# Rows of a modulation, sums of u and sigmoids moved between the stages of a decoder block's token mixer

## The chip, the cores and the metric

The kernel runs on one NeuronCore of a Trainium2 chip. Its time is the device time of one execution in microseconds (us). Five engines work side by side, each with its own queue in program order: PE (TensorE, matmuls; PEld loads their weights), DVE (VectorE, elementwise work on two operands), ACT (ScalarE, copies and functions with one operand), POOL (GpSimd) and SP (SyncE, which issues the DMAs here). Semaphores tie the queues together. On-chip data lie in SBUF, and matmuls write to eight PSUM banks of 128 x 512 floats.

## The reference

A decoder block of width 1024 over 512 tokens: a first SwiGLU network, a token mixer and a second SwiGLU network, each behind an RMSNorm with a modulation that a vector c sets (shift, scale and gate, nine vectors of 1024 in all), then a last RMSNorm. What matters here:

```python
mod = cond @ w_ada[l] + b_ada[l]                      # 9 x 1024 values, 72 groups of 128
sh1, sc1, gt1, sh2, sc2, gt2, sh3, sc3, gt3 = ...
u = modulate(rmsnorm(h, g_norm_mix[l]), sh2, sc2)
h = h + gt2 * token_mixing(u, ...)
...
def token_mixing(u, ...):
    proj = u @ w_in                                   # p (256), q, k, v (768 each), gate logits (2 x 1024)
    y_pool = multiscale_pool(p, w_pool, pool_scale)   # trailing means over 2, 4, 8, 16 tokens
    # rotary q and k; three groups of four heads: window 128, and dilations 4 and 16
    y_attn = ...                                      # merged by the groups' softmax denominators
    gates = jax.nn.sigmoid(gate_logits)
    g_pool, g_attn = jnp.split(gates, 2, axis=-1)
    merged = g_pool * (y_pool @ w_pool_branch) + g_attn * (y_attn @ w_attn_branch)
    return merged @ w_out
```

## The kernel before

Activations lie feature by feature on the partitions: u is eight tiles of 128 features x 512 tokens. Every matmul is done in three: each fp32 operand is split into a high part (rounded to the fp32r format, a copy on ACT) and a low part (the difference, on DVE), and high x high, high x low and low x high are summed (`mm3`, L360 to L362). So each weight chunk of 128 x 1024 that SP loads into a buffer (`raw`, three of them) costs ACT an instruction (L317, into `whi`) and DVE one (L329, into `wlo`). PE runs without a break almost everywhere; DVE is the next busiest. Nothing is scheduled by a planner: the order on each engine is the order in which the Python code records instructions. Work for DVE and ACT is put beside PE's matmuls by hooks, called ahead of the k-th step of a product tile (`mm_tile`, eight steps of three matmuls).

The mixer (`mix`, `merge_out`) goes through these stages, in PE's order:

- first values: four tiles of v for the first head group, with the rotary steps (`rope_b`, L1058 and L1059) of the first q and k beside them; the shifted copies for these are made by DMAs from `v23` (L1050);
- eight product tiles of q and k for the groups two and three, with attention units of the first group in their hooks at step 5: values (L1147), transposes of the probabilities (L1129), scores (L1096), and DVE's and ACT's softmax (`at_exp`, L1112 to L1117);
- two tiles for the pooling, whose trailing sums POOL makes (`pool_diff`, L1219 to L1228);
- values by class: four tiles, one for each residue class of the tokens (L1380 to L1382), each copied from its bank into `v23` by DVE (L1386), with the units of groups two and three in their hooks at step 5. The unit's values (L1147) in the tile of class c+1 read the copy of class c;
- four gate tiles (output tiles 6 and 7, gates for pooling and attention), and beside them the merge of the groups' softmax (`at_merge`), pooling's map (`pool_map`) and the attention's output (`at_spread` on PE, `at_y` on DVE and ACT);
- the gated merge (`merge_out`): for each output tile a branch of 12 matmuls (`branch`) and, for six of the eight, the gates by pairs in a product of the Strassen kind with seven products of 24 narrow matmuls instead of eight (`gate_duo`, L747 to L749);
- output product: five full tiles, then three in two halves of the tokens (`out_tail`), in which the sums of squares for the next norm are gathered in `AR` (L440, L557) and read by PE (`stats_t`, L450).

Three kinds of work are spread over these stages and matter here.

A row of the modulation: 512 KB of `w_ada` are loaded into a free tile (`ada_fetch`, L379), and DVE multiplies it with the condition and sums it up in one instruction of 128 x 1024 (`ada_do`, L387). `bg` does one row and fetches ahead by `ada_depth`; every eight rows a group is closed by one or two small instructions (`ada_fin`, L400 to L404). Rows 48 to 63 are done in the mixer up to the values by class (`ada_stop` 64), 64 to 71 in the output product.

Sums of u: the seven products need sums and differences of u's four quarters, split in two parts again. `mix_sums` returns them as a list of steps that `nxt` takes off one at a time: L977 adds two parts, L987 subtracts, L981 (ACT) and L985 (DVE) split. Its scratch tiles x are q and k tiles that are free late.

Sigmoids: the four gate tiles stay in PSUM, and `merge_out` applies the sigmoid to all four at one point (`sigmoids`, L1487), with ACT's table load ahead of them.

In the duo the first product's bank A is copied on ACT to C and reused (L1407); PE's third and fifth product, which add to A, wait for such copies.

Of the kernel before, what the change touches and what calls it, by code (L numbers as in the profile page):

```python
# [14 lines left out]
P = 128  # L15
T = 512
# [130 lines left out]
class Kernel:  # L147
# [234 lines left out]
    def ada_do(self, j, n=1, between=None):  # L382
        t, mod = self.adat.pop(j), self.mod[:, j:j + 1]
        for i in range(n):
            c = slice(i * D // n, (i + 1) * D // n)
            o = self.part if i else mod
            self.nc.vector.scalar_tensor_tensor(t[:, c], t[:, c], 1.0, self.cond[:, c], op0=OP.mult, op1=OP.mult,  # L387
                                                accum_out=o)
# [4 lines left out]
        if self.ada_free is not None and not any(t is x for x in self.ada_gone):  # L393
            self.ada_free.append(t)
# [799 lines left out]
    def at_y(self, banks):  # L1194
        nc, v = self.nc, self.nc.vector
        for hp in range(2):
            x, y = self.o1[:, hp, :], self.o23[:, hp, :]
            v.tensor_tensor(x, x, banks[2 * hp], op=OP.mult)
            v.tensor_tensor(y, y, banks[2 * hp + 1], op=OP.mult)
            v.tensor_tensor(x, x, y, op=OP.add)  # L1200
            nc.scalar.activation(self.YH[hp], x, AF.Copy)
            v.tensor_tensor(self.YL[hp], x, self.YH[hp], op=OP.subtract)
# [28 lines left out]
    def pool_map(self):  # L1231

        nc = self.nc
        banks = (self.bO, self.bS[0])
# [10 lines left out]
    def mix(self):  # L1245
# [7 lines left out]
        two = lambda pool, n, dt=F32R: [pool.tile([P, T], dt, name=f"{n}{i}") for i in range(2)]  # L1253
        self.PH, self.PL, self.YH, self.YL = (two(mp, n) for n in ("PH", "PL", "YH", "YL"))
        ma = outer.enter_context(tc.tile_pool(name="ma", bufs=1))
        with tc.tile_pool(name="rt", bufs=1) as self.rt, tc.tile_pool(name="aw", bufs=2) as self.aw, \
# [19 lines left out]
            self.ada_free, self.ada_stop, self.ada_depth = [self.AR], 64, 2  # L1276
# [15 lines left out]
            for n in range(4):  # L1292
# [59 lines left out]

            self.ada_gone = mine
            self.ada_free = [x for x in self.ada_free if not any(x is y for y in mine)] + [self.cs]
            self.ada_depth = 1
            b = self.mm_tile(hooks(g23[0], [(2, lambda: by_class(1)), (3, self.bg), (7, self.bg)]))
            self.pool_diff(1, b)
            wide = lambda pool, n: lambda: pool.tile([P, D], F32R, name=n)
# [7 lines left out]
            sums, last = self.mix_sums([self.qt[2], self.qt[1], self.kt[1]], [[wide(ma, "k2"), wide(mp, "uc")],  # L1366
                                       [wide(ma, "v1"), wide(ma, "k0")], [lambda: half(0), lambda: half(1)]])
            nxt = lambda: sums.pop(0)()
            self.held = self.pos
            w = [x for _ in range(4) for x in self.take()]  # L1370
            for c in range(4):
                mid = [lambda c=c: by_class(c + 1)] if c in (1, 2) else []
                hk = hooks(g23[c + 1], [(7, self.bg)], mid) if c < 3 else \
                    hooks([], [(2, self.at_swap), (2, nxt), (3, nxt), (6, nxt), (7, nxt)])
                b = self.nb()
                for k in range(KT):
# [6 lines left out]
                    if k == 4:  # L1383
# [4 lines left out]
            assert self.ada_next == 64 and not self.adat, self.ada_next  # L1388
            gates = [self.mm_tile(hooks([], [(1, nxt), (3, nxt), (5, self.at_merge)]))]
            v.memset(self.fT.bitcast(F32), 0.0)  # L1390
            v.tensor_tensor(self.sel.rearrange("p (j d) -> p j d", j=8),
                            *(self.ident[:64, r:r + 8, None].to_broadcast([64, 8, 64]) for r in (0, 32)), op=OP.add)
            gates.append(self.mm_tile({1: [nxt], 3: [nxt], 6: [self.pool_map, lambda: self.at_fT(self.bS[1])]}))
# [7 lines left out]
        self.merge_out(gates, last, ma)  # L1401
# [42 lines left out]
    def merge_out(self, ready, last, ma):  # L1444
        nc, tc = self.nc, self.tc
        v = nc.vector
        with tc.tile_pool(name="mg", bufs=1) as mg:
# [15 lines left out]
            def branch(m):  # L1463
                gp, ga = (x[:, m % 2 * T:(m % 2 + 1) * T] for x in sc)
                self.look()
# [13 lines left out]
                def parts():  # L1479
                    nc.scalar.activation(MH[m], gp, AF.Copy)  # L1480
# [4 lines left out]
            def sigmoids():  # L1485
                for i, b in enumerate(ready):
                    nc.scalar.activation(sc[i % 2][:, i // 2 * T:(i // 2 + 1) * T], b, AF.Sigmoid)  # L1487


            rest = [sigmoids]  # L1490
            do = lambda n=1: [rest.pop(0)() for _ in range(n)]

            place(tile_of(ma, "q1"), 6)
            place(tile_of(ma, "k1"), 7)
# [34 lines left out]
            for m in range(5):  # L1529
# [6 lines left out]
                self.bg()  # L1536
                if m < 3:
                    self.bg()
# [7 lines left out]
    def build(self):  # L1546
# [39 lines left out]
        self.ada_free, self.ada_depth, self.ada_gone = None, 3, []  # L1586
# [189 lines left out]
```

## Time and profile before

| | |
|---|---|
| Median of 3 runs | 995.04 us (992.8 to 995.55) |
| The profiled execution | 994.62 us, of which the span from the first to the last instruction is 992.8 |
| Granted TensorE clock | 1.000 |
| PE busy | 981.1 us, 99% of the span |
| DVE busy | 787.2 us, 79% |
| ACT busy | 475.3 us, 48% |
| POOL busy | 32.3 us, 3% |
| The mixer in the span | from about 360 to 645 us |
| POOL's sums | 452 to 480 us |

How to read the rows: a timeline row gives the start in us from the span's start, the time in us, engine, line, operation, out<-in by the program's names, shapes, and in brackets the engine's idle time before it and what ended it. The next instruction of DVE can start some 0.08 us before the row of the last one ends. A row of the waits view gives who waited for whom: us in total, times, longest. A row of the DMA view ends with the median us from issue to landing. `bank` stands for any PSUM bank, and `k`, `q`, `v`, `uc` for tiles of that name, which later hold other things (sums of u, merged halves).

### The profile page before, as it was taken

How to read it: one execution, taken by the hardware profiler on the slowest of the kernel's cores; microseconds unless marked ns; L12 is line 12 of the kernel's file. 1: busy time of each engine (PE TensorE's matmuls, PEld its weight loads, DVE VectorE, ACT ScalarE, POOL GpSimd, SP SyncE). 2: the span in 40 equal slices, each digit the busy share in tenths (PEclk: the TensorE clock that was granted, in tenths of full speed). 3: DMA queues.
4: the chain of work that ended last, by engine and by line, in shares of the span. 5: the costliest groups of instructions: out<-in, count | busy, mean ns of one | idle time of the engine just before them, and what ended most of it. 6: DMA issues, size and time to landing. Idle time of an engine off the chain costs nothing.

```text
span 992.8 us, 16356 instructions
## 1 busy us (share of the span) xinstructions
PE 981.1 (99%) x6686; PEld 893.3 (90%) x6686; DVE 787.2 (79%) x1091; ACT 475.3 (48%) x713; POOL 32.3 (3%) x31
## 2 busy tenths in 40 slices
PE   8999999999999999999999999999999999999997
PEld 7888998989999899787878998998899899998997
DVE  7989979889797676889888876868787776676764
ACT  6453653625435554455535553455365254352553
POOL 0000000000000000007300000000000000000002
PEclk9999999999999999999999999999999999999999
DMA  9856446455563415655133325522344134241312
GB/s 344 277 187 236 150 149 193 147 194 169 182 197 111 135 56 194 195 198 199 61 101 114 104 67 195 190 64 90 103 152 133 55 111 144 85 150 43 105 45 85
DMA packets 44876, 141.74 MB, mean 143 GB/s; under 512 B 6273, under 2 KB 9089, under 8 KB 44802
## 3 DMA queue, kind: packets, MB, share of 16 engines
q1 hardware_dynamic: 44226, 140.18, 43.4%
q8 instruction: 52, 0.85, 0.4%
q10 hardware_dynamic: 576, 0.52, 0.2%
q14 instruction: 22, 0.18, 0.1%
HBM read 135.29 MB, written 2.24 MB: 139 GB/s over the span
## 4 chain that ended last, share of the span: by engine, by line
PE 87%; DVE 6%; ACT 2%; issue 2%; DMA 2%; SPq 0%; POOL 0%; POOLq 0%; DVEq 0%; ACTq 0%
PE bank L360 14%; PE bank L361 14%; PE bank L362 14%; PE bank L747 13%; PE bank L748 12%; PE bank L749 12%; PE bank L1702 1%; PE bank L1704 1%; PE bank L1706 1%; DVE wlo L329 1%; DMA H<-xT 1%; DVE ut L467 1%; PE bank L1147 1%; DVE UL L493 1%; PE bank L1096 0%
## 5 line engine op out<-in xcount | busy, mean ns | idle before, releaser
L329 DVE TENSOR_TENSOR wlo<-raw,whi 128x1024 fp32r<-128x1024 f32 (+4 forms) x162 | 172.8, 1079 | 49.7 <-ACT whi L317 49.4
L747 PE MATMUL bank<-UH,whi 128*128 128x256 f32 x640 | 176.8, 276 | 0.0
L748 PE MATMUL bank<-UL,whi 128*128 128x256 f32 x640 | 176.8, 276 | 0.0
L749 PE MATMUL bank<-UH,wlo 128*128 128x256 f32 x640 | 176.8, 276 | 0.0
L317 ACT ACTIVATE whi<-raw 128x1024 fp32r<-128x1024 f32 (+4 forms) x162 | 146.3, 921 | 57.6 <-DVE raw L261 54.1
L360 PE MATMUL bank<-HI,whi 128*128 128x512 f32 (+1 forms) x406 | 146.2, 360 | 0.0
L361 PE MATMUL bank<-HK,whi 128*128 128x512 f32 (+1 forms) x406 | 145.9, 359 | 0.0
L362 PE MATMUL bank<-HI,wlo 128*128 128x512 f32 (+1 forms) x406 | 145.8, 359 | 0.0
L329 DVE TENSOR_TENSOR wlo<-X,whi 128x1024 fp32r<-128x1024 f32 (+3 forms) x104 | 112.0, 1084 | 31.8 <-ACT whi L317 31.5
L747 PEld LDWEIGHTS bank<-UH,whi 128*128 128x128 f32 x640 | 120.2, 188 | 0.4
L748 PEld LDWEIGHTS bank<-UL,whi 128*128 128x128 f32 x640 | 120.2, 188 | 0.0
L749 PEld LDWEIGHTS bank<-UH,wlo 128*128 128x128 f32 x640 | 120.2, 188 | 0.0
L747 PE MATMUL bank<-SH,whi 128*128 128x256 f32 x408 | 112.7, 276 | 0.0
L748 PE MATMUL bank<-SL,whi 128*128 128x256 f32 x408 | 112.6, 276 | 0.0
L749 PE MATMUL bank<-SH,wlo 128*128 128x256 f32 x408 | 112.6, 276 | 0.0
L317 ACT ACTIVATE whi<-X 128x1024 fp32r<-128x1024 f32 (+3 forms) x104 | 95.7, 943 | 34.4 <-DVE X L261 33.7
L360 PE MATMUL bank<-UH,whi 128*128 128x512 f32 (+1 forms) x304 | 105.6, 347 | 0.0
L361 PE MATMUL bank<-UL,whi 128*128 128x512 f32 (+1 forms) x304 | 104.2, 343 | 0.1
L362 PE MATMUL bank<-UH,wlo 128*128 128x512 f32 (+1 forms) x304 | 104.0, 342 | 0.0
L362 PEld LDWEIGHTS bank<-HI,wlo 128*128 128x128 f32 x406 | 76.2, 188 | 11.7
L360 PEld LDWEIGHTS bank<-HI,whi 128*128 128x128 f32 x406 | 76.2, 188 | 11.5
L361 PEld LDWEIGHTS bank<-HK,whi 128*128 128x128 f32 x406 | 76.3, 188 | 11.3
(336 smaller groups left out, 1842.4 us busy)
## 6 DMA issues: line engine op xcount, KB each, us to landing
raw<-wmix SPq DMA_DIRECT2D x44, 512.0 KB, 3.8
raw<-wf1i SPq DMA_DIRECT2D x31, 512.0 KB, 4.3
raw<-wf2i SPq DMA_DIRECT2D x30, 512.0 KB, 4.4
ada<-wada SPq DMA_DIRECT2D x23, 512.0 KB, 5.7
AR<-wada SPq DMA_DIRECT2D x18, 512.0 KB, 4.6
cs<-wada SPq DMA_DIRECT2D x14, 512.0 KB, 3.7
X<-wf2i SPq DMA_DIRECT2D x14, 512.0 KB, 3.7
X<-wf1i SPq DMA_DIRECT2D x12, 512.0 KB, 4.3
```

The costliest lines, as they stand in the source:

```text
L317: self.nc.scalar.activation(self.hi[:, y], r[:, x], AF.Copy)
L329: self.nc.vector.tensor_tensor(self.lo[:, y], r[:, x], self.hi[:, y], op=OP.subtract)
L360: M(ps, hi, uh, start=start, stop=False)
L361: M(ps, hi, ul, start=False, stop=False)
L362: M(ps, lo, uh, start=False, stop=stop)
L467: self.nc.vector.scalar_tensor_tensor(t[:, hs], self.H[k][:, hs], G, self.Rn[hs.start][:, hs], op0=OP.mult, op1=OP.mult)
L493: self.nc.vector.scalar_tensor_tensor(self.UL[k][:, hs], t[:, hs], S, self.UH[k][:, hs], op0=OP.add, op1=OP.subtract)
L747: M(o, hi, uh, start=start and p == 0 and k == 0, stop=False, skip_group_check=True)
L748: M(o, hi, ul, start=False, stop=False, skip_group_check=True)
L749: M(o, lo, uh, start=False, stop=k == 3, skip_group_check=True)
L1147: self.nc.tensor.matmul(self.bO[64 * h:64 * h + 64, P * hp:P * hp + P], x, pt[:, (2 * h + j) * P:(2 * h + j + 1) * P], start=j == first, s ...
L1702: M(b, hi, self.UH[k], start=k == 0, stop=False)
```

## The change

It does four things.

1. Rows. A tile `uc` is added to the free tiles for the first rows, and one row is done beside each of the last three of the four first values (three rows instead of one). The mixer stops at row 61 instead of 64: the eight q and k tiles keep one row each and the first pooling tile two, and the rows in the second pooling tile (two) and in the first three classes (one each) are gone. The output product does 11 rows (3, 3, 2, 2, 1 beside its full tiles) instead of 8 (2, 2, 2, 1, 1).
2. Sums of u. They start in the second pooling tile instead of the fourth class: two steps there, two each in the first and second class, three in the fourth, and one or two in the gate tiles. Their scratch is three tiles of the pool `mx` that later hold PH, YH and YL (so these become two halves of one tile), and q2. The constants for the spread (`fT`, `sel`) are made beside the third class.
3. Sigmoids. Each gate tile has its sigmoid beside a later gate tile; the result goes into q1 and k1, and the merge of output tiles 6 and 7 reads it from there. The tiles for the merged halves 6 and 7 are placed when they are written.
4. `at_y` makes both high parts before both low parts.

PE's instructions and their order are the same in both kernels.

```diff
     def mix_sums(...):
         def last():
-            u = x[0].rearrange("p (k t) -> p k t", k=4)
+            u = x[3].rearrange("p (k t) -> p k t", k=4)
...
-        return [lambda: whole(b, 0, 1), lambda: whole(x[0], 4, 1),
-                lambda: (v.tensor_tensor(x[0], x[0], b, op=OP.add), hi(0)), lambda: whole(x[1], 0, 0),
-                lambda: sub(x[2], x[1], b), lambda: (sub(x[1], x[0], x[1]), lo(0)),
-                lambda: (hi(2), whole(x[0], 4, 0)), lambda: (hi(1), sub(x[0], x[0], x[1])), lambda: lo(2), lambda: lo(1)], last
+        return [lambda: whole(b, 0, 1), lambda: whole(x[0], 4, 1), lambda: v.tensor_tensor(x[0], x[0], b, op=OP.add),
+                lambda: whole(x[1], 0, 0), lambda: sub(x[2], x[1], b), lambda: sub(x[1], x[0], x[1]),
+                lambda: (hi(0), whole(x[3], 4, 0)), lambda: lo(0), lambda: sub(x[3], x[3], x[1]), lambda: hi(1),
+                lambda: hi(2), lambda: lo(2), lambda: lo(1)], last
...
     def at_y(self, banks):
...
             nc.scalar.activation(self.YH[hp], x, AF.Copy)
-            v.tensor_tensor(self.YL[hp], x, self.YH[hp], op=OP.subtract)
+        for hp in range(2):
+            v.tensor_tensor(self.YL[hp], self.o1[:, hp, :], self.YH[hp], op=OP.subtract)
...
     def mix(self):
+        x = [mp.tile([P, D], F32, name=n) for n in ("PH", "YL", "YH")]
...
-            self.ada_free, self.ada_stop, self.ada_depth = [self.AR], 64, 2
+            uf = mp.tile([P, D], F32, name="uc")
+            self.ada_free, self.ada_stop, self.ada_depth = [self.AR, uf], 61, 2
...
+                if n == 1:
+                    self.ada_free += [self.v23.rearrange("p n f -> p (n f)")[:, i * D:(i + 1) * D] for i in range(2)]
+                if n:
+                    self.bg()
                 if n == 2:
-                    mine = [self.v23.rearrange("p n f -> p (n f)")[:, i * D:(i + 1) * D] for i in range(2)]
-                    self.ada_free += mine
-                    self.bg()
+                    self.ada_free = [t for t in self.ada_free if t is not uf]
...
-            b = self.mm_tile(hooks(g23[0], [(2, lambda: by_class(1)), (3, self.bg), (7, self.bg)]))
+            sums, last = self.mix_sums(x + [self.qt[2]], ...)
+            b = self.mm_tile(hooks(g23[0], [(2, lambda: by_class(1)), (3, nxt), (7, nxt)]))
...
-                hk = hooks(g23[c + 1], [(7, self.bg)], mid) if c < 3 else \
-                    hooks([], [(2, self.at_swap), (2, nxt), (3, nxt), (6, nxt), (7, nxt)])
+                hk = hooks(g23[c + 1], [(2, nxt), (7, nxt)] if c < 2 else [(2, clear)], mid) if c < 3 else \
+                    hooks([], [(2, self.at_swap), (2, nxt), (3, nxt), (6, nxt)])
...
-            gates = [self.mm_tile(hooks([], [(1, nxt), (3, nxt), (5, self.at_merge)]))]
-            v.memset(self.fT.bitcast(F32), 0.0)
-            v.tensor_tensor(self.sel...)
+            gates = [self.mm_tile(hooks([], [(5, self.at_merge), (7, nxt)]))]
...
-            gates.append(self.mm_tile({1: [nxt], 3: [nxt], 4: [lambda: self.at_spread(spread)]}))
+            at = [t[:, i * T:(i + 1) * T] for t in (self.qt[1], self.kt[1]) for i in range(2)]
+            sig = lambda i: lambda: nc.scalar.activation(at[i], gates[i], AF.Sigmoid)
+            gates.append(self.mm_tile({1: [nxt, sig(0)], 2: [sig(1)], 4: [lambda: self.at_spread(spread)]}))
             self.at_y(spread)
-            gates.append(self.mm_tile())
+            gates.append(self.mm_tile({1: [sig(2)]}))
+            sig(3)()
...
     def merge_out(...):                 # branch(m)
+                sp, sa = (gp, ga) if m < 6 else (ready.pop(0), ready.pop(0))
...
-                    v.tensor_tensor(gp, gp, pb, op=OP.mult)
-                    v.tensor_tensor(ga, ga, ab, op=OP.mult)
+                    v.tensor_tensor(gp, sp, pb, op=OP.mult)
+                    v.tensor_tensor(ga, sa, ab, op=OP.mult)
...
-            rest = [sigmoids]
+            rest = []
...
                 self.sumsq(m, self.H[m])()
-                self.bg()
-                if m < 3:
+                for _ in range((3, 3, 2, 2, 1)[m]):
                     self.bg()
```

L996 of the changed kernel, which the prediction names, is the third step of `mix_sums` there, the sum of x[0] and b.

More of the change, by code (lines that the diff above doesn't have):

```diff
@@ L392, in ada_do @@
                 between()
-        if self.ada_free is not None and not any(t is x for x in self.ada_gone):
+        if self.ada_free is not None:
             self.ada_free.append(t)
@@ L1229, in pool_diff, with pool_map @@
         self.pd[t] = d
-    def pool_map(self):
+    def pool_map(self, high, low):
         nc = self.nc
+        self.PH, self.PL = high, low
         banks = (self.bO, self.bS[0])
@@ L1252, in mix @@
         mp = outer.enter_context(tc.tile_pool(name="mx", bufs=1))
-        two = lambda pool, n, dt=F32R: [pool.tile([P, T], dt, name=f"{n}{i}") for i in range(2)]
-        self.PH, self.PL, self.YH, self.YL = (two(mp, n) for n in ("PH", "PL", "YH", "YL"))
+        x = [mp.tile([P, D], F32, name=n) for n in ("PH", "YL", "YH")]
+        two = lambda n: [t[:, i * T:(i + 1) * T] for t in [mp.tile([P, D], F32R, name=n)] for i in range(2)]
+        wide = lambda pool, n: lambda: pool.tile([P, D], F32R, name=n)
         ma = outer.enter_context(tc.tile_pool(name="ma", bufs=1))
@@ L1351, in mix @@
             self.pool_diff(0, b)
-            self.ada_gone = mine
-            self.ada_free = [x for x in self.ada_free if not any(x is y for y in mine)] + [self.cs]
-            self.ada_depth = 1
-            b = self.mm_tile(hooks(g23[0], [(2, lambda: by_class(1)), (3, self.bg), (7, self.bg)]))
-            self.pool_diff(1, b)
-            wide = lambda pool, n: lambda: pool.tile([P, D], F32R, name=n)
+            assert self.ada_next == 61 and not self.adat, self.ada_next
             v4 = []
@@ L1364, in half, with clear @@
                 return v4[0][:, i * D:(i + 1) * D]
-            sums, last = self.mix_sums([self.qt[2], self.qt[1], self.kt[1]], [[wide(ma, "k2"), wide(mp, "uc")],
+            sums, last = self.mix_sums(x + [self.qt[2]], [[wide(ma, "k2"), wide(mp, "uc")],
                                        [wide(ma, "v1"), wide(ma, "k0")], [lambda: half(0), lambda: half(1)]])
             nxt = lambda: sums.pop(0)()
+            b = self.mm_tile(hooks(g23[0], [(2, lambda: by_class(1)), (3, nxt), (7, nxt)]))
+            self.pool_diff(1, b)
             self.held = self.pos
             w = [x for _ in range(4) for x in self.take()]
+            def clear():
+                v.memset(self.fT.bitcast(F32), 0.0)
+                v.tensor_tensor(self.sel.rearrange("p (j d) -> p j d", j=8),
+                                *(self.ident[:64, r:r + 8, None].to_broadcast([64, 8, 64]) for r in (0, 32)), op=OP.add)
             for c in range(4):
                 mid = [lambda c=c: by_class(c + 1)] if c in (1, 2) else []
-                hk = hooks(g23[c + 1], [(7, self.bg)], mid) if c < 3 else \
-                    hooks([], [(2, self.at_swap), (2, nxt), (3, nxt), (6, nxt), (7, nxt)])
+                hk = hooks(g23[c + 1], [(2, nxt), (7, nxt)] if c < 2 else [(2, clear)], mid) if c < 3 else \
+                    hooks([], [(2, self.at_swap), (2, nxt), (3, nxt), (6, nxt)])
                 b = self.nb()
@@ L1387, in mix @@
             self.held = None
-            assert self.ada_next == 64 and not self.adat, self.ada_next
-            gates = [self.mm_tile(hooks([], [(1, nxt), (3, nxt), (5, self.at_merge)]))]
-            v.memset(self.fT.bitcast(F32), 0.0)
-            v.tensor_tensor(self.sel.rearrange("p (j d) -> p j d", j=8),
-                            *(self.ident[:64, r:r + 8, None].to_broadcast([64, 8, 64]) for r in (0, 32)), op=OP.add)
-            gates.append(self.mm_tile({1: [nxt], 3: [nxt], 6: [self.pool_map, lambda: self.at_fT(self.bS[1])]}))
+            gates = [self.mm_tile(hooks([], [(5, self.at_merge), (7, nxt)]))]
+            pool_map = lambda: self.pool_map(two("PH"), two("PL"))
+            gates.append(self.mm_tile({1: [nxt], 3: [nxt], 6: [pool_map, lambda: self.at_fT(self.bS[1])]}))
             rest = [b for b in self.banks if b not in gates] + [self.bS[0]]
@@ L1584, in build @@
         self.scr2 = dram.tile([32, 2 * T], F32, name="scr2")
-        self.ada_free, self.ada_depth, self.ada_gone = None, 3, []
+        self.ada_free, self.ada_depth = None, 3
         with self.open_ffn():
```

10 lines of the change are left out of this document (4 added, 6 removed).

## The prediction

> **What bounds the kernel now.** I read the page first, then PE's waits between 420 and 680 us (the stretch that the change touches), then the rows around each wait, engine by engine.
>
> ```profile
> span 992.8 us, 16356 instructions
> PE 981.1 (99%) x6686; PEld 893.3 (90%) x6686; DVE 787.2 (79%) x1091; ACT 475.3 (48%) x713; POOL 32.3 (3%) x31
> ...
> PE bank L747 <- ACT bank L1407: 1.3, 1, 1.3
> PE bank L1147 <- DVE v L1386: 0.8, 1, 0.8
> PE bank L747 <- ACT gc L1407: 0.6, 1, 0.6
> ```
>
> PE is busy for 99% of the span, so only PE's own waits can be won, and any new wait of PE is paid in full. In this stretch there are three of note, and behind each stands DVE's queue, directly or through ACT. PE runs the same 6501 instructions in the same order in both kernels; the change moves DVE, ACT and SP instructions against them.
>
> ```profile
> 469.90 1.09 PE L1147 MATMUL bank<-probT,v 128*64 128x128 f32 x16 [0.85 <-DVE v L1386]
> ...
> 526.69 0.28 PE L747 MATMUL bank<-k,whi 128*128 128x256 f32 x1
> ...
> 529.30 0.28 PE L749 MATMUL bank<-k,wlo 128*128 128x256 f32 x1
> 530.92 0.39 PE L747 MATMUL bank<-v,whi 128*128 128x256 f32 x1 [1.35 <-ACT bank L1407]
> 531.14 0.28 PE L748 MATMUL bank<-k,whi 128*128 128x256 f32 x1
> ...
> 533.73 0.28 PE L749 MATMUL bank<-v,wlo 128*128 128x256 f32 x1
> ...
> 536.56 0.28 PE L749 MATMUL bank<-UH,wlo 128*128 128x256 f32 x1
> 537.45 0.39 PE L747 MATMUL bank<-v,whi 128*128 128x256 f32 x1 [0.61 <-ACT gc L1407]
> ```
>
> Counted from start to start, the second wait costs 529.30 to 530.92 less one step, 1.5 us, the third 536.56 to 537.45 less one step, 0.8. A wait also leaves a slower beat: 23 steps from 526.69 to 529.30 are 0.1135 each, 22 from 531.14 to 533.73 are 0.1177. Over the five products of 24 narrow matmuls that follow in this duo that is another 0.5.
>
> **The duo's waits (gain).** What made DVE and ACT late there:
>
> ```profile
> 511.65 0.63 ACT L1201 ACTIVATE YH<-o 128x512 fp32r<-128x512 f32 x1 [5.55 <-DVE o L1200]
> 520.06 1.28 ACT L1487 ACT_TABLE_LOAD   x1
> ...
> 523.28 1.08 ACT L317 ACTIVATE whi<-cs 128x1024 fp32r<-128x1024 f32 x1
> ...
> 528.71 1.15 ACT L317 ACTIVATE whi<-raw 128x512 fp32r<-128x512 f32 x2 [3.40 <-DVE raw L261]
> ...
> 530.29 0.58 ACT L1407 ACTIVATE bank<-bank 128x512 f32<-128x512 f32 x1
> ...
> 518.18 0.39 PE L362 MATMUL bank<-UH,wlo 128*128 128x512 f32 x1
> ...
> 524.39 1.23 DVE L329 TENSOR_TENSOR wlo<-cs,whi 128x1024 fp32r<-128x1024 f32 x1 [3.05 <-ACT whi L317]
> 527.46 1.22 DVE L261 TENSOR_TENSOR raw<-raw,raw 128x1024 f32<-128x1024 f32 x1
> ```
>
> Table load and four sigmoids hold ACT from 520.06 to 523.28, between the high part of AR and that of cs. DVE waits 3.05 us for the latter, so its raw<-raw comes at 527.46, ACT's high part at 528.71, and the copy of A's bank, which PE needs at 529.4, ends at 530.87. After the change the table load and two sigmoids fall into ACT's 5.55 us of idle time before 511.65; the other two stand ahead of AR's high part, and the last waits for the last gate tile, whose matmuls end at 518.6. So AR's high part goes from 519.0 to about 519.3, but that of cs from 523.28 to about 520.3, and the whole chain behind it comes 2.9 us earlier: raw<-raw at 524.6, the copy ends at 528.0. PE no longer waits at 529.4, and the third wait's copy comes 2.9 earlier against 2.3 that PE itself gains, a margin of about 0.4. The low parts YL, now behind both halves, no longer wait for ACT each; that lies ahead of the same chain and isn't counted again. Gain 1.5 + 0.8 + 0.5 = 2.75, the upper bound; the lower is 1.5, if the third wait stays. Fewer sums in the gate tiles give nothing of their own: the output of the attention there waits for PE's spread matmuls.
>
> **First values (loss).** Three modulation rows instead of one stand here. The last rotary step, which the first scores read, now has two rows ahead of it instead of one.
>
> ```profile
> 392.31 0.69 DVE L1059 TENSOR_TENSOR k<-k,k 128x512 f32<-128x512 f32 x1
> ...
> 393.57 0.71 PE L1096 MATMUL bank<-k,q 64*128 64x128 f32 x8
> ...
> 396.72 0.39 ACT L1117 ACTIVATE prob<-prob,negmax 128x128 f32<-128x128 f32 x1
> ...
> 399.80 0.60 PE L1129 MATMUL bank<-cst,prob 128*128 128x128 f32 x4
> ...
> 611.83 1.22 DVE L387 SCALAR_TENSOR_TENSOR k<-k,cond 128x1024 f32<-128x1024 f32 x1
> ...
> 612.97 1.22 DVE L387 SCALAR_TENSOR_TENSOR k<-k,cond 128x1024 f32<-128x1024 f32 x1
> ```
>
> A row costs DVE 1.14 from start to start (611.83 to 612.97). The rotary step ends at 393.00, 0.57 before PE's scores; handing over takes 0.14 (a copy of v ends at 469.76, PE starts at 469.90). So 1.14 - 0.43 = 0.7 us of new wait; bounds 0 and 1.1. DVE is then 2.3 late, PE 0.7; the probabilities have 2.7 us until their transposes (397.11 to 399.80), which covers the difference of 1.6, and DVE's waits for loads and scores up to 440 take it up. The two loads more on SP's queue stand before and among the shifted copies, long before they are used; the weights' first load behind them stays first.
>
> **Values by class (loss).** Five rows leave, and u's sums come in their place, one for one, but for one: in the first class a sum at its third step (L996) is added ahead of the copy of v that PE waits for already.
>
> ```profile
> 462.46 3.47 DVE L329 TENSOR_TENSOR wlo<-raw,whi 128x1024 fp32r<-128x1024 f32 x2 [1.46 <-ACT whi L317]
> ...
> 469.08 0.68 DVE L1386 COPY v<-bank 128x512 f32<-128x512 f32 x1
> ...
> 476.48 0.68 DVE L1386 COPY v<-bank 128x512 f32<-128x512 f32 x1
> ...
> 462.67 2.17 POOL L1228 TENSOR_TENSOR k<-k,tr 64x512 f32<-64x512 f32 x1
> ...
> 474.10 1.29 POOL L1228 TENSOR_TENSOR k<-k,v 64x512 f32<-64x512 f32 x1
> ...
> 478.82 0.44 PE L1147 MATMUL bank<-probT,v 128*64 128x128 f32 x4
> ```
>
> DVE's queue is full from 462.46 to that copy, and its idle 1.46 before can't take the sum, which stands behind the low part that waits for ACT. So the copy comes later by at least 1.14. Beside POOL such an instruction took up to 2.3 us (two low parts 3.47, of which 1.2 is what one takes alone), and POOL's own was stretched from 1.29 to 2.17: they take turns. With one more DVE instruction there, the low part behind it meets POOL's next one. I take 2.0, nearer the slow rows since POOL has work at nearly every moment there; bounds 1.1 and 3.2.
>
> [...]
>
> In the second class two sums replace one row: 1.14 against 478.82 - 477.16 - 0.14 = 1.5 of slack, so nothing; one more turn of POOL's would make it 0.6 to 0.8. From there on DVE has less to do than before, and POOL's differences, later too, are read only in the gate tiles.
>
> **Output product (loss).** Eleven rows instead of eight stand here, all ahead of the last sum of squares of the first half, which PE reads at 639.99, and with them the two small instructions that close the group of the first 64 rows.
>
> ```profile
> 611.16 0.75 DVE L1534 SCALAR_TENSOR_TENSOR H<-bank,mod,H 128x512 f32<-128x512 f32 x1 [4.60 <-PE bank L362]
> ...
> DVE AR L440 <- ACT ut L439: 2.9, 4, 0.8
> ...
> 632.68 0.09 DVE L387 DVE_READ_ACCUMULATOR k<-k,cond 128x1 f32 x1
> ...
> 633.08 0.48 DVE L516 SCALAR_TENSOR_TENSOR H<-bank,mod,H 128x256 f32<-128x256 f32 x1
> ...
> 638.40 0.42 DVE L557 TENSOR_TENSOR AR<-AR,gc 128x256 f32<-128x256 f32 x1
> ...
> 639.99 0.60 PE L450 MATMUL bank<-ones,AR 128*128 128x128 f32 x4
> ...
> k<-wada SPq DMA_DIRECT2D x6, 512.0 KB, 6.2
> ```
>
> From 611.16, where PE released it, to 638.82 DVE waits for nothing but four times for ACT's square of its own result (2.9 us together, and these waits stay). Three rows are 3.4 us, the closing pair 0.4 (its like stands between 632.68 and 633.08). The slack at the sum is 639.99 - 638.82 - 0.14 = 1.0. PE waits 2.8; with 0.1 for a row whose load is late, 2.9. A load needs 6.2 us in the median and three tiles rotate, so at three rows a tile one may be 1.5 late: bounds 1.5 and 4.4. The weights' loads behind the rows on SP's queue come 2 to 3 us later, but ACT's use of them is later by as much.
>
> **Sum.** 994.62 (the profiled execution; its span 992.8 and 1.8 around it) + 0.7 + 2.0 + 2.9 - 2.75 = 997.5 us, 0.25% over the median 995.04, which lies 0.4 over the profiled one. All other work is the same. A measurement of this kernel can tell about 0.3% (3.0 us) from no change, so the sum is a loss just inside it. From the bounds: 994.62 + 0 + 1.1 + 1.5 - 2.75 = 994.5 to 994.62 + 1.1 + 4.0 + 4.4 - 1.5 = 1002.6.
>
> **Rivals.**
> A, faster: DVE takes the added work in its own waits (2.9 before L440, 1.46 before 462.46). Then no new wait arises and the by-class one of 0.85 goes with its rows: 994.62 - 2.75 - 0.85 = 991.0. Against it: those waits stand behind instructions fixed in order.
> B, the output product's rows are hidden: the sum is done before PE asks, which needs 2.8 of 3.8 us found elsewhere. 997.5 - 2.9 = 994.6. For it: DVE idles for 4.6 us before 611.16; against it: the rows stand behind that instruction.
> C, slower: POOL's turns. If in the first two classes L996 and the sums behind it each wait out one POOL instruction (about 1.0 each), both copies of v are late: by-class 2.0 becomes 3.2, the second class adds 0.8, and 0.5 more where the third follows. 997.5 + 2.5 = 1000.0. It decides from the second extra turn on. For it: the row of 3.47; against it: with the first class later, POOL is nearly done when the second comes.
> D, the change doesn't do what it says: the fourth sigmoid waits for the last gate tile ahead of AR's high part. If that delay is 3 us rather than 0.3, the copies come as late as now: 997.5 + 2.75 = 1000.2.
> E, PE's clock falls after the longer waits (2.9 each, at the first class and at the sum of squares). The granted clock is 1.00 in every row, beside a wait of 1.35 too. At half rate for as long as each wait lasts, 1.45 each: 1000.4. [...]
>
> **Chances.** Forecast 0.46, its own range 995.5 to 999.2, of which the part over 998.0 (0.15) is slower and the rest (0.31) the same. A 0.12, B 0.12, C 0.19, D 0.07, E 0.04. Faster: A less a sliver, 0.11. Same: 0.31 + 0.12 + 0.01 = 0.44. Slower: 0.15 + 0.19 + 0.07 + 0.04 = 0.45. The range 993.0 to 1001.0 holds the forecast and B to E and leaves out A and the outer ends of C and E, about 0.17.
>
> **What would show it.** PE's wait before the values of the second class grows from 0.85 to 2.9; the two waits on L1407's copies are gone and the beat stays at 0.1135; a new wait of 2.8 stands before L450, released by DVE's L557; one of 0.7 before the first L1096. It is wrong if L450 or the first class shows no new wait (then A or B), if a copy of A's bank still holds PE (D), or if the granted clock leaves 1.00 (E).

## The result and the profile after

The changed kernel takes 996.36 us in the median against 994.15 for the kernel before, both over 22 runs: a ratio of 1.0023, with a 95% interval of 1.0016 to 1.0029. It is 2.2 us slower, which is inside the 0.3% that count as no change here. The forecast was 997.5. The profiled execution took 995.25, only 0.63 more than that of the kernel before, so 1.6 of the 2.2 isn't in this first trace; it is looked for below.

The page of the changed kernel, its span and PE's row:

```profile
span 993.5 us, 16359 instructions
PE 981.3 (99%) x6686; PEld 893.9 (90%) x6686; DVE 787.3 (79%) x1091; ACT 475.3 (48%) x713; POOL 33.9 (3%) x31
```

PE's waits between 380 and 680 us (what waits, for what, us in all, how often, the longest):

```profile
PE bank L450 <- DVE AR L557: 2.6, 1, 2.6
PE bank L1147 <- DVE v L1396: 0.9, 1, 0.9
...
```

Busy times are nearly the same; the waits have moved. Both waits on ACT's copies in the duo are gone, the one before the values of the second class has kept its size, and a new one of 2.6 stands before L450. The rows behind this, from the timeline (start, duration, instruction; in brackets the wait before it and who ended it):

```profile
393.85 0.69 DVE L1059 TENSOR_TENSOR k<-k,k 128x512 f32<-128x512 f32 x1
393.98 1.11 PE L1096 MATMUL bank<-k,q 64*128 64x128 f32 x8
...
470.76 1.09 PE L1147 MATMUL bank<-probT,v 128*64 128x128 f32 x16 [0.90 <-DVE v L1396]
...
519.45 0.60 ACT L1406 ACTIVATE k<-bank 128x512 f32<-128x512 f32 x1 [3.06 <-PE bank L362]
...
520.89 1.05 ACT L317 ACTIVATE whi<-cs 128x1024 fp32r<-128x1024 f32 x1
...
528.06 0.58 ACT L1419 ACTIVATE bank<-bank 128x512 f32<-128x512 f32 x1
530.14 0.28 PE L749 MATMUL bank<-k,wlo 128*128 128x256 f32 x1
530.25 0.28 PE L747 MATMUL bank<-v,whi 128*128 128x256 f32 x1
...
640.07 0.42 DVE L557 TENSOR_TENSOR AR<-AR,gc 128x256 f32<-128x256 f32 x1
640.54 0.71 PE L450 MATMUL bank<-ones,AR 128*128 128x128 f32 x4 [2.59 <-DVE AR L557]
```

- First values: the eight scores take 1.11 from the first to the end instead of 0.71. The first four start on time, since they read the earlier rotary step; the other four wait for the one that ends at 394.54.
- Duo: the last sigmoid waits for its gate tile and ends at 520.05; the high part of cs starts at 520.89 instead of 523.28, though PE is 0.84 later there than in the kernel before (the first three rows of the table below). The copy of A's bank ends at 528.64, and PE goes from 530.14 to 530.25 without a break.
- Output product: the last sum of squares ends at 640.49, and PE has been idle since 638.0.

PE runs the same 6686 matmuls in the same order in both kernels (the 6501 of the prediction stands in no view), so one can subtract the starts of the same instruction. How much later (+) PE gets through each stretch, from the profiled executions; the third and fourth columns compare further executions (e1 and e4, below) with the first one of the changed kernel:

| stretch of the kernel before, us | changed - before | e1 - changed | e4 - changed |
|---|---|---|---|
| 0 to 390 (start, first network) | +0.41 | -0.68 | -0.55 |
| 390 to 400 (first values) | +0.40 | 0.00 | 0.00 |
| 400 to 529 (values by class, gate tiles) | +0.03 | -0.01 | +0.02 |
| 529 to 600 (duos) | -3.03 | 0.00 | 0.00 |
| 600 to 645 (output product) | +2.81 | +1.59 | +2.15 |
| 645 to the end | +0.01 | +0.03 | 0.00 |
| sum | +0.63 | +0.93 | +1.62 |

The first row is no part of the change: the start differs by such amounts between executions (by 0.2 between two of the kernel before, by 0.7 between two of the changed one). The rest sums to +0.22, far from the 2.2 of the medians.

### The profile page after: what moved, and what is told of

Read it like the earlier page. It is cut to its first block, busy times and chain, and to the rows that moved or that the text cites. A ratio compares the mean times of both kernels' runs of the same rounds, so it can differ in the third digit from the quotient of the medians.

```text
span 993.5 us, 16359 instructions
## 1 busy us (share of the span) xinstructions
PE 981.3 (99%) x6686; PEld 893.9 (90%) x6686; DVE 787.3 (79%) x1091; ACT 475.3 (48%) x713; POOL 33.9 (3%) x31
## 4 chain that ended last, share of the span: by engine, by line
PE 83%; DVE 8%; DMA 3%; SPq 2%; ACT 2%; issue 2%; POOL 0%; POOLq 0%; DVEq 0%; ACTq 0%
PE bank L747 13%; PE bank L748 13%; PE bank L749 13%; PE bank L360 12%; PE bank L361 12%; PE bank L362 12%; DVE wlo L329 2%; SPq L1050 1%; PE bank L1710 1%; PE bank L1712 1%; PE bank L1714 1%; DMA v<-wada 1%; DMA rt<-tr 1%; DVE k L387 1%; DVE v L387 1%
```

## The experiments

Eleven runs. e1 to e4 stood beside runs of the kernel before with a median of 994.33, e5 to e8 beside 994.74, e9 to e11 beside 994.46.

**e1: the changed kernel again.**

> The changed kernel unaltered, for a second profiled execution. Question: the two traces shown differ by 0.63 us at PE's end, the medians by 2.2. If the profiled execution was only a quick one of the same kind (theory: no cost is missing, the executions vary), this one shows PE's waits at the same places with the same sizes (0.9 before the values of the second class, 2.6 before L450) and a ratio of about 1.0022. If a cost is missing from that trace (rival: the granted clock falls after the wait of 2.6 in most executions, since most ran at a mean clock of 0.997 and this profile at 0.999), a profile with a mean clock of 0.997 shows a stretch of a clock under 1.00 behind L450 and 1 to 2 us of slower matmuls there.

997.39, ratio 1.0029 (1.0019 to 1.0040). All waits are where they were, with the wait before L450 at 2.5. But behind it PE is slower. Windows of 1 us of this execution (length, PE's busy time and matmuls, granted clock, share of the DMA engines, GB/s):

```profile
639.00:640.00 1.00, 0.19 (x1) 1.00 0.63 205
640.00:641.00 1.00, 1.00 (x10) 0.99 0.87 266
641.00:642.00 1.00, 1.00 (x7) 0.50 0.69 131
642.00:643.00 1.00, 1.00 (x6) 0.50 0.78 311
643.00:644.00 1.00, 1.00 (x7) 0.50 0.13 53
644.00:645.00 1.00, 1.00 (x9) 0.80 0.00 0
645.00:646.00 1.00, 1.00 (x10) 1.00 0.42 25
```

The windows behind the same wait in the first execution of the changed kernel:

```profile
640.00:641.00 1.00, 0.46 (x4) 1.00 0.75 164
641.00:642.00 1.00, 1.00 (x11) 1.00 0.69 274
642.00:643.00 1.00, 1.00 (x11) 1.00 0.63 250
643.00:644.00 1.00, 1.00 (x11) 1.00 0.71 291
```

In e1 the clock stands at half from 640.98 to 644.40 (worked out from 0.99 and 0.80 in the end windows), 3.42 us, and 6 or 7 matmuls go through in a microsecond instead of 11. That is the +1.59 of the table. e4, below, has the same fall, from 640.4 to 643.8. The mean clock of an execution is a sign of it: 0.997 or less in 17 of the 22 runs of the result and in all 8 of e1, never under 0.998 in the 63 runs of the kernel before beside the experiments. It is a rough sign: the clock also falls at the end of a trace (from 992.26 of 992.8 in the kernel before, from 991.43 of 993.5 in the changed one, worked out from windows of 0.2 us), and the profiled execution of e8, below, has a mean of 0.998 with 1.00 in every window from 635 to 647. The rival holds: this cost was missing from the first trace.

**e2: three rows early.** DVE is idle from 604.4 to 609.0 ahead of the first product's result, and the first loads have landed by then.

```diff
             do()
+            for _ in range(3):
+                self.bg()
             bs = [self.nb(), self.nb()]
...
-                for _ in range((3, 3, 2, 2, 1)[m]):
+                for _ in range((2, 2, 2, 1, 1)[m]):
```

> Three of the eleven rows of the output product stand ahead of its first product's read, in DVE's idle stretch from 604.4 to 609.0 (three rows take 3.4; the third load landed at 606.8), eight behind as before the change. Theory (the three extra rows are the whole of the new wait before L450): that wait of 2.6 is gone or under 0.3, 2.7 us less than the changed kernel, 993.7, ratio 0.9995 to the kernel before; if the clock falls because of that wait, another 1 less, 992.7 (0.9985). Rival (the wait comes from ACT's squares or the loads that come late behind the rows): the wait stays at 1.5 or more, ratio above 1.001.

991.93, ratio 0.9973 (0.9962 to 0.9984): 4.4 less than the changed kernel in the result, 5.5 less than e1 on the same chip, and 2.4 less than the kernel before beside it. The timeline of e2:

```profile
603.73 1.22 DVE L387 SCALAR_TENSOR_TENSOR k<-k,cond 128x1024 f32<-128x1024 f32 x1
...
606.02 1.22 DVE L387 SCALAR_TENSOR_TENSOR v<-v,cond 128x1024 f32<-128x1024 f32 x1
...
608.41 0.75 DVE L1545 SCALAR_TENSOR_TENSOR H<-bank,mod,H 128x512 f32<-128x512 f32 x1 [0.76 <-PE bank L362]
...
636.48 0.41 DVE L557 TENSOR_TENSOR AR<-AR,gc 128x256 f32<-128x256 f32 x1
637.24 0.60 PE L450 MATMUL bank<-ones,AR 128*128 128x128 f32 x4
```

The three rows end before PE's result comes, DVE even waits 0.76 for it, and L557 ends 0.35 before PE asks. PE wins 2.81 over this stretch against the first trace of the changed kernel, exactly what the stretch had lost, and no run of e2 has a mean clock under 0.998: with the wait the fall is gone. That is more than the 2.7 of the first theory, and near what its second half allowed (992.7).

**e3 and e4: one half of the duo's edits undone.** e3 puts the sigmoids behind the last gate tile again, e4 each low part behind its high part.

```diff
-            gates.append(self.mm_tile({1: [nxt, sig(0)], 2: [sig(1)], 4: ...
+            gates.append(self.mm_tile({1: [nxt], 4: ...
...
-            gates.append(self.mm_tile({1: [sig(2)]}))
-            sig(3)()
+            gates.append(self.mm_tile())
...
-        self.merge_out(at, last, ma)
+        self.merge_out(list(at), last, ma, lambda: [sig(i)() for i in range(4)])
...
-            rest = []
+            rest = [sigs]
```

> The changed kernel with its four sigmoids behind the last gate tile again; all else stays. Theory (the sigmoids between the high parts of AR and of cs made the copies of A's bank late): the waits of 1.5 and 0.8 before L747 and the slower beat between them are back, 2.7 to 3.0 us, 999.2, ratio 1.005. Rival (the order of the low parts YL, which no longer wait for ACT one by one, took the waits away): no wait over 0.3 there, ratio 1.0022 as the changed kernel.

```diff
             nc.scalar.activation(self.YH[hp], x, AF.Copy)
-        for hp in range(2):
-            v.tensor_tensor(self.YL[hp], self.o1[:, hp, :], self.YH[hp], op=OP.subtract)
+            v.tensor_tensor(self.YL[hp], x, self.YH[hp], op=OP.subtract)
```

> The changed kernel with each low part YL right behind its high part again; the sigmoids stay with their tiles. Theory (the sigmoids alone do it): no wait over 0.3 before L747, ratio 1.0022 as the changed kernel. Rival (the order of the low parts does it): waits of 1 to 2.5 us before L747, ratio 1.004 to 1.005.

e3: 997.94, ratio 1.0032 (1.0020 to 1.0043). e4: 996.86, ratio 1.0022 (1.0013 to 1.0031). Times at this spread settle little here; the traces do. PE's wait on L1407's copy (L1418 there) in e3, and the copy of A's bank there:

```profile
PE bank L747 <- ACT gc L1418: 0.6, 1, 0.6
...
528.64 0.58 ACT L1418 ACTIVATE bank<-bank 128x512 f32<-128x512 f32 x1
```

Only the second of the two waits is back. Against the kernel before, the duos of e3 are still 1.8 shorter, so the order of the low parts alone does that much: the copy of A's bank ends at 529.22 instead of 530.87. Undoing the sigmoids costs 1.2, not the 2.7 to 3.0 of the theory, and the rival's "no wait over 0.3" fails as well. e4 has no wait there: its duos take what those of the changed kernel take. The two edits cover each other.

**e5: both undone**, on top of e2.

> Base is the kernel with three rows early (e2, 991.93), where no wait before L450 and no fall of the clock blurs small terms. Here the sigmoids stand behind the last gate tile and each low part YL right behind its high part, both as before the change. Theory (either of the two takes the first wait of the duo away by itself, so undoing one alone showed little; together they are the gain): both waits before L747 are back, 1.5 and 0.8, with the slower beat, 2.8 to 3.0, 994.9. Rival (the gain came from something else, such as the earlier outputs of the attention or fewer sums in the gate tiles): the waits stay away, or come to under 1.5 together, 992 to 993.4.

994.75, ratio 0.9997 (0.9989 to 1.0006). PE's waits in e5:

```profile
PE bank L747 <- ACT bank L1417: 1.3, 1, 1.3
PE bank L747 <- ACT gc L1417: 0.8, 1, 0.8
```

Both are back, and PE loses 2.7 between 529 and 545 against e2. The two edits together are the gain, nearly all of it.

**e6: one sum less ahead of the copy of v**, on top of e2. L996 stands at the seventh step instead of the third, in the place of the next sum, and each later sum moves one place; so L996 itself is still ahead of the copy, and the sum after it goes behind.

```diff
-                hk = hooks(g23[c + 1], [(2, nxt), (7, nxt)] if c < 2 else [(2, clear)], mid) if c < 3 else \
-                    hooks([], [(2, self.at_swap), (2, nxt), (3, nxt), (6, nxt)])
+                hk = hooks(g23[c + 1], ([(7, nxt)], [(2, nxt), (7, nxt)], [(2, clear)])[c], mid) if c < 3 else \
+                    hooks([], [(2, self.at_swap), (2, nxt), (3, nxt), (6, nxt), (7, nxt)])
```

> Base is e2 (991.93). The sum L996 leaves the first class's third step, and each later sum moves one place back, so that four stand beside the last class. Theory (the wait of 0.9 before the values of the second class is made of that sum, 1.17 us ahead of the copy of v): the wait is gone, 0.9 less, 991.0. Rival (the turns with POOL set the copy, and without L996 the low part behind it waits out POOL's instruction all the same): the wait stays at 0.5 or more, 991.5 to 991.9.

991.81, ratio 0.9970 (0.9959 to 0.9981). In the trace the wait of 0.9 before L1147 is gone, and PE wins 0.94 there against e2. The medians don't show that: against the kernel before, e6 is at 0.9970 and e2, on another chip, at 0.9973.

**e7: one row beside the first values**, on top of e2; rows 59 and 60 go to the last two classes.

```diff
-            uf = mp.tile([P, D], F32, name="uc")
-            self.ada_free, self.ada_stop, self.ada_depth = [self.AR, uf], 61, 2
+            self.ada_free, self.ada_stop, self.ada_depth = [self.AR], 59, 2
...
-                if n == 1:
+                if n == 2:
                     self.ada_free += ...
-                if n:
                     self.bg()
-                if n == 2:
-                    self.ada_free = [t for t in self.ada_free if t is not uf]
...
+            self.ada_free, self.ada_stop, self.ada_depth = [self.AR], 61, 1
+            self.bg_fetch()
...
-                hk = hooks(g23[c + 1], ... [(2, clear)], mid) if c < 3 else \
-                    hooks([], [(2, self.at_swap), (2, nxt), (3, nxt), (6, nxt)])
+                hk = hooks(g23[c + 1], ... [(2, clear), (7, self.bg)], mid) if c < 3 else \
+                    hooks([], [(2, self.at_swap), (2, nxt), (3, nxt), (6, nxt), (7, self.bg)])
```

> Base is e2 (991.93). One row beside the first values, as before the change; the two others stand beside the last two classes. Theory (the new wait before the first scores, 0.45, and the wait of 0.9 before the values of the second class cover each other: what PE loses at the first gives DVE time at the second): the first wait is gone, the second grows by as much, to 1.3, and the time stays at 991.9. Rival (the two add, as the prediction had it): the first is gone, the second stays at 0.9, 991.4.

992.47, ratio 0.9978 (0.9968 to 0.9987), not to be told from e2. In the trace PE wins 0.40 at the first scores, and the second class gives back 0.1 of it. The rival, that the two terms add, is nearly right; that one covers the other falls.

**e8: one row early instead of three** (1 and (2, 3, 2, 2, 1) in e2's diff).

> The changed kernel with one row of the output product instead of three ahead of the first product's read; ten stand behind it. PE's wait before L450 becomes 2.6 - 1.1 = 1.5. Theory A (the clock falls to half for some 3 us only where a wait is long enough, and 1.5 is too short): mean clock 0.999 in all executions, 991.93 + 1.5 = 993.4. Theory B (any wait of more than 1 us can bring it): most executions at 0.997, 994.5 to 995.

994.41, ratio 0.9996 (0.9988 to 1.0005). The wait before L450 is 1.5, as expected. Three of eleven runs have a mean clock of 0.997 (995.7 on average), the others more (994.2). So neither theory: at 1.5 the mean clock is low in a few. The profiled run isn't one of them, so no trace shows where the clock falls in those.

**e9: e2, e6 and e7 together** (here too one sum less ahead of the copy of v, as in e6).

> e2 with both further steps: L996 behind the copy of v (e6) and one row instead of three beside the first values, the two others beside the last two classes (e7). Theory (the three terms stand apart, each a wait of PE of its own): no wait of PE over 0.4 between 390 and 680 us, 0.9 + 0.3 less than e2, 990.8; ratio to the kernel before 0.996. Rival (two rows beside the last classes bring a wait of their own there, or DVE's time won at the first values is what took the wait at the second class away): 991.5 to 992.

991.06, ratio 0.9967 (0.9955 to 0.9980), 0.3% faster than the kernel before, the fastest of the study and near the theory's 990.8. PE wins 0.40 at the first scores and 0.94 at the second class, and the longest wait of PE between 360 and 680 us is this:

```profile
PE bank L460 <- DVE r L455: 0.4, 1, 0.4
```

**e10: the kernel before again.**

> The kernel before, unaltered, for a second profiled execution. Question: the wait of 0.85 before the values of the second class is there without L996, and e6, which has sums instead of rows and no L996 there, has none. Theory (in the kernel before, the step that makes negmax at 458.57 takes 1.30 instead of 0.17, because POOL's L1228 holds it, and ACT's exponentials and high parts come that much later; a standing trait of the order of instructions): the same step takes over 1 us again and the wait is 0.7 to 1.0. Rival (a chance of that one execution): the step takes 0.17 and the wait is under 0.3.

994.31, ratio 0.9999 (0.9988 to 1.0009). The step for negmax takes 1.30 again and the wait before L1147 is 0.9; the rows are shown in the next section.

**e11: a longer wait.** Two more instructions of DVE, whose result nothing reads, behind the last row of the output product.

```diff
+                for t in self.ada_free[:2] if m == 4 else ():
+                    v.tensor_tensor(t, t, self.cond, op=OP.mult)
```

> The changed kernel with two more DVE instructions of 1.14 each behind the last row of the output product (their result is not read; the outputs are the reference's). PE's wait before L450 becomes 2.6 + 2.3 = 4.9. Theory (whether the clock falls hangs on how much of a fixed stretch the wait fills; at 1.5 it fell in a few executions, at 2.6 in most): it falls in every execution, mean clock 0.997 or less, the fall in the profile lasts 3.3 or a whole multiple of it, 996.8 + 2.3 = 999.1 or up to 1 more. Rival (the fall is a matter of chance alone, about 8 in 10 whatever the wait): some executions at 0.999, 998 in the median.

999.22, ratio 1.0047 (1.0031 to 1.0062); all four runs at 0.997 or less. The wait is 5.1. Windows of e11, as above:

```profile
638.00:639.00 1.00, 0.06 (x1) 1.00 0.00 0
...
640.00:641.00 1.00, 0.00 (x0) 0.91 0.87 205
...
642.00:643.00 1.00, 0.00 (x0) 0.50 0.51 119
...
644.00:645.00 1.00, 1.00 (x7) 0.50 0.85 184
...
646.00:647.00 1.00, 1.00 (x7) 0.50 0.21 82
647.00:648.00 1.00, 1.00 (x8) 0.67 0.00 0
648.00:649.00 1.00, 1.00 (x12) 1.00 0.00 0
```

The fall lasts from 640.82 to 647.66, 6.84 us, twice the 3.42 of e1. A third of it meets a PE that waits anyway, until 643.1. Four of four is too few to rule out a chance of 8 in 10; two things speak against a chance that is the same whatever the wait: the doubled length, and the 3 of 11 in e8 behind a wait of 1.5.

## Why the prediction was right or wrong

The time was right, 997.5 against 996.36, and so was its sign, but in part by luck. Two of its terms were right; the other two errors nearly cancel: a term of 2.0 that isn't there, and a fall of the clock of 1.6, in most executions, that stood among the rivals.

| term | forecast | trace | the runs that show it |
|---|---|---|---|
| first values | +0.7 | +0.40 | e7: -0.40 without the two rows |
| values by class | +2.0 | +0.03 | e6, e10 |
| output product, the wait | +2.9 | +2.8 | e2: gone with three rows moved |
| duo | -2.75 | -3.0 | e5: +2.7 with both edits undone |
| clock behind the wait | rival E, 0.04 | +1.6 (e1), in about 8 of 10 executions | e1, e4, e11; none in e2 |

Working out the median from the traces: 0.40 + 0.03 - 3.0 + 2.8 = 0.2 for the waits, and 1.6 in 17 of 22 executions, 1.2 on average, makes 1.4 of the 2.2, or 1.7 with the 1.9 that the fall costs in e4 beside its longer wait. What is left, 0.5 to 0.8, stays open. It isn't a matter of the fall alone: the five executions of the result at 0.998 or 0.999 are at 995.4 on average, 1.2 over the kernel before, where the waits explain 0.2.

**First values.** The step was right and the size too large: the prediction let all eight scores wait for the last rotary step, and only four read it.

**Output product.** Right by its own steps: three rows and the closing pair, against a slack of 1.0. Moved ahead of L1543, the same rows cost nothing. Rival B named DVE's idle 4.6 us as cover and rejected it because the rows stand behind that instruction; e2 shows that this position was the whole cost. "ACT's squares" as the cause of the wait, and late loads, fall with e2 too.

**Duo.** The gain came as worked out. What the prediction didn't count is that the new order of the low parts is worth 1.8 by itself (e3). It "isn't counted again" in the text because it lies ahead of the same chain, which was right for the sum. Of the three parts of the gain, the slower beat is the one that the runs bear out least: in e5 both waits are back, but the 22 steps from 531.42 to 533.93 are 0.114 each and not 0.1177, and PE loses 2.7 instead of 3.0. So a wait doesn't by itself leave a slower beat; what does stays open. (1.5 + 0.8 + 0.5 is 2.8, not 2.75.)

**Values by class: the step that failed.** "In the first class a sum at its third step (L996) is added ahead of the copy of v" is true, and its price was nearly right; that the rest of the chain stays was wrong. Rows of the second profiled execution of the kernel before (e10), DVE's with one of POOL and one of ACT:

```profile
458.36 1.30 POOL L1228 TENSOR_TENSOR k<-k,tr 64x512 f32<-64x512 f32 x1
458.40 1.30 DVE L1114 TENSOR_SCALAR negmax<-st 128x2 f32<-128x2 f32 x1
459.61 1.21 DVE L387 SCALAR_TENSOR_TENSOR AR<-AR,cond 128x1024 f32<-128x1024 f32 x1
459.73 0.51 ACT L1117 ACTIVATE prob<-prob,negmax 128x256 f32<-128x256 f32 x1 [0.48 <-DVE negmax L1114]
...
462.28 3.46 DVE L329 TENSOR_TENSOR wlo<-raw,whi 128x1024 fp32r<-128x1024 f32 x2 [1.46 <-ACT whi L317]
...
468.89 0.68 DVE L1386 COPY v<-bank 128x512 f32<-128x512 f32 x1
```

The same place in the changed kernel:

```profile
459.31 0.17 DVE L1114 TENSOR_SCALAR negmax<-st 128x2 f32<-128x2 f32 x1
459.38 2.34 DVE L977 TENSOR_TENSOR PH<-UH,UL 128x1024 f32<-128x1024 f32 x1
462.17 1.23 DVE L329 TENSOR_TENSOR wlo<-raw,whi 128x1024 fp32r<-128x1024 f32 x1 [0.44 <-ACT whi L317]
463.31 1.25 DVE L996 TENSOR_TENSOR PH<-PH,cs 128x1024 f32<-128x1024 f32 x1
463.56 2.15 POOL L1229 TENSOR_TENSOR k<-k,tr 64x512 f32<-64x512 f32 x1
464.48 2.32 DVE L329 TENSOR_TENSOR wlo<-raw,whi 128x1024 fp32r<-128x1024 f32 x1
...
469.94 0.68 DVE L1396 COPY v<-bank 128x512 f32<-128x512 f32 x1
```

And in e6, where L996 stands in the place of the next sum:

```profile
459.31 0.17 DVE L1114 TENSOR_SCALAR negmax<-st 128x2 f32<-128x2 f32 x1
...
462.17 2.39 DVE L329 TENSOR_TENSOR wlo<-raw,whi 128x1024 fp32r<-128x1024 f32 x2 [0.47 <-ACT whi L317]
...
466.96 1.21 DVE L996 TENSOR_TENSOR PH<-PH,cs 128x1024 f32<-128x1024 f32 x1
468.10 0.68 DVE L1396 COPY v<-bank 128x512 f32<-128x512 f32 x1
```

From the start of negmax to the copy it is 10.49 in the kernel before, 10.63 in the changed one and 8.79 in e6. So one sum more ahead of the copy costs 1.84: 1.17 of its own and 1.1 because the low part behind L996, which starts while POOL's L1229 runs (463.56 to 465.71), takes 2.32 instead of 1.23, less 0.4 by which later steps are quicker. The prediction took 2.0, an estimate between 1.1 and 3.2; no run shows that term, and in its place the runs show 1.84 for the sum and +0.03 for the stage. L996 itself isn't held (1.25), though L1229 starts within it; only the low part is.

But sums in place of rows had won 1.70 at the same place (10.49 less 8.79). 1.0 of it lies at negmax. In the kernel before, negmax takes 1.30 and ends with POOL's L1228; ACT's exponentials and then its high parts wait for it, and DVE waits 1.46 for those. In the changed kernel and in e6 negmax takes 0.17, and the sum behind it takes 2.34 instead, which nothing on that chain reads; DVE then waits 0.44. Another 1.1 lies at the two low parts, 3.46 in the kernel before (3.47 in its first trace, beside POOL's L1228 of 2.17) and 2.39 in e6; later steps give 0.4 back. The prediction priced the instruction that was added and left the times around it as they were.

Why negmax is held in the one kernel and not in the other wasn't tried, and stays open; e10 shows only that it is a standing trait. A start inside a running instruction of POOL isn't enough for it: the negmax step before this one starts so in both kernels, at 457.69 in the first trace of the kernel before (POOL's L1226, 455.94 to 458.27) and at 458.43 in the changed kernel (L1227, 456.69 to 459.04), and takes 0.61 there (0.60 in e10) and 0.17 here. That the copy is late by the old amount again is also why rival A was half right: the wait of 0.85 does go with its rows, and L996 brings one of the same size back.

**The clock.** Rival E had the half rate and one of its two places, the wait before L450. The rate of 0.50 stands in e1, e4 and e11, and in the trace of the kernel before too, but only behind its last matmul, from 992.26 to the end. E let the fall last as long as the wait, at a cost of 1.45; it lasts 3.42 behind waits of 2.5 (e1) and 2.8 (e4) and 6.84 behind one of 5.1 (e11), and costs 1.6 in e1. Its evidence against, a granted clock of 1.00 behind a wait of 1.35, didn't reach to 2.6. The first trace of the changed kernel is one of the executions without the fall, so taken alone it would have refuted E wrongly.

## What to carry to other kernels

When work is moved to a late stage, look for the last idle time of its engine ahead of the consumer that PE waits for: the same three instructions cost 2.8 us of wait and most often 1.6 of a slower clock behind a result that comes from PE, and nothing ahead of it. Where DVE's instructions take longer beside POOL's (the low part 2.32 instead of 1.23 here), price a replaced instruction by the chain after the replacement, not by adding its length. When medians and traces disagree, profile the same kernel again and compare the mean clock of all runs before looking for another cause.

## What the hardware showed that was not expected

A wait of PE can bring a clock at half that lasts longer than the wait: 3.42 us at 0.50 behind 2.5 us in e1, and none in e2, where the wait is gone. Behind waits of 2.5 to 2.8 the mean clock fell to 0.997 or less in 37 of 47 runs (the result, e1, e3, e4), behind 1.5 in 3 of 11 (e8), behind 5.1 in 4 of 4; the waits of 1.3 in the duo did it in none of the 63 runs of the kernel before.

The fall doesn't begin with the end of the wait. In e1 it begins 1.2 us after PE has started again (639.81, as the 0.19 of the first window of e1 says, against 640.98), in e11 at 640.82, 2.3 us before PE starts again, and there it lasts twice as long as in e1 and e4. Nor does the length of the wait alone decide: 2.5 in e1 and 2.8 in e4 brought a fall, 2.6 in the first trace of the changed kernel and in that of e3 brought none (1.00 in every window from 636 to 647). What decides, and what sets the length of the fall, was not shown.
